# A hybrid convolution and RWKV-7 block on one Trainium2 core: scan products in one array shape, the state on VectorE, the forward substitution on GpSimd

## The chip, the cores and the metric

The kernel runs on one core of one Trainium2 chip. A core has TensorE (PE in the profile), VectorE (DVE), ScalarE (ACT), GpSimd (POOL) and SyncE (SP, here only a queue of DMA issues). Each engine works through its own instructions in the order in which they were put there, and waits for another engine at a semaphore. The metric is the device time of one execution in microseconds, the median of several runs.

## The reference

The input is x, 512 tokens of 1024 channels; 16 learned meta tokens are put ahead, so 528 tokens run through one layer of float32 arithmetic:

```python
p = h @ w_in                                  # GLU columns | r, k, v, low-rank downs | two gates
A = conformer_conv(p[:, :2048])               # GLU, causal depthwise convolution (31 taps), LN, swish, projection
B = rwkv7_time_mix(p[:, 2048:5408])           # scan, per head: S = S diag(w) + (S a) b^T + v k^T ;  y = S r
h = LN(alpha * h + (sigmoid(gA) * A + sigmoid(gB) * B) @ w_o)
h = LN(alpha * h + conv_gated_mlp(h))         # up 2 x 2816, depthwise convolution (3 taps), gate, down
```

The scan has 16 heads of 64 values. In it a is the normalised key with a minus sign, and b the normalised key times a learned rate.

## The kernel before, in words

Every large product is a `gemm` (lines 157 to 162): weights and activations are split into a high and a low part, and three products are accumulated for each of eight 128-row slices, at L160, L161 and L162. Weights come by SP's DMA queue (L146); ScalarE makes the high part (L137), VectorE the low one (L140, tile wl).

The scan runs over eight pairs of heads, and in a pair over nine chunks of 64 tokens; chunk 0 holds the 16 meta tokens. `rkv` (part K) projects r, k and v of a pair. `prep` (part P) forms decays, the matrices AR and BK, the squared norms of the keys (nsc, tokens on partitions) and the scores Gt of each chunk (L408, masked at L409). A score product contracts over the 64 channels of one head, so it has 64 rows by 128 columns of the array; the profile prints that as 64*128. ScalarE then scales Gt by the key norms (L412). The decay and rate products of the low-rank weights wup (L336, L346) also use 64 rows each.

`solve` (part S) inverts a triangular matrix for every chunk. The blocks go through DRAM (dA) into one block per partition, L and W. VectorE makes 31 steps of two instructions each (L475 a product, L477 a sum), and each needs the one before; 15 single instructions do the same for chunk 0 (L481). Between dependent steps the code puts instructions of the depthwise convolution (L647, L655). The result goes back through DRAM (dT). `merge` (L499 on) transposes a block (L512) and makes the remaining block with two sets of TensorE products (L517, L522). `chain` (L525 on) then goes through the chunks in order; every step has products of TensorE at L530 and evictions of ScalarE: R (L548), UV (L552), the state St (L559) and Y (L564). The state is decayed by one more product with the identity matrix. `finish` normalises the output, `glu` and `gate` are more gemms, and `conv` is the depthwise convolution on VectorE.

The string `SCHEDULE` lists the parts in the order in which they are put to a scheduler, for instance `C0 K2 F0 G2 S12`: `S12` is the solve of pair 1 with the convolution of tile 2 between its steps. The scheduler settles one fixed order of instructions per engine before anything runs. `front()` gives the chain and evictions a high priority, `back()` a low one. PSUM has three banks for gemms (ps_g), two for the chain (ps_x), two for scores and transposes (ps_a) and one for the rest (ps_m).

## Time and profile before

| | before |
|---|---|
| three runs, us | 1223.47, 1225.12, 1210.57 (median 1223.47) |
| profiled execution, us | span 1223.2 |
| PE busy | 1186.4 us, 97% |
| DVE busy | 844.0 us, 69% |
| ACT busy | 605.0 us, 49% |
| POOL busy | 60.8 us, 5% |
| stage with the scans, 100 to 640 us | PE 534.91 of 540.00 us |

The profiled execution takes as long as the median run: its span of 1223.2 us is 0.3 us below it. A matmul that starts while the one ahead is still draining counts as busy in both, so PE's share says little of how dense its work is; starts of successive matmuls do. A float32 product is two records in the trace, a gemm product one. The times of matmuls are given with the array shape that they use (128*128, 64*128, 64*64) and the moving tile.

### The profile page before, as it was taken

Reading aid. Unit: us, or ns where it says so; the run is one execution under the profiler, and the core shown is the slowest. Engines: PE = TensorE matmul, PEld = TensorE weight load, DVE = VectorE, ACT = ScalarE, POOL = GpSimd, SP = SyncE. Lnnn points to the kernel's source line nnn. Section 1 sums busy time; section 2 is a strip of 40 time slices with the busy share of each in tenths; the row PEclk is TensorE's granted clock in tenths of the full one; section 3 lists DMA queues with packets and bytes.
Section 4 is the critical chain, followed back from the end, with each engine's and each line's share of the span. In section 5 each row is a group of like instructions: output and inputs, shape, how many; then the busy total and the mean of one; then the engine's idle time right before and its main releaser. Section 6 shows DMA issues by size and latency. Waiting matters only on the chain.

```text
span 1223.2 us, 22803 instructions
## 1 busy us (share of the span) xinstructions
PE 1186.4 (97%) x8790; PEld 1079.5 (88%) x8790; DVE 844.0 (69%) x2103; ACT 605.0 (49%) x1407; POOL 60.8 (5%) x204
## 2 busy tenths in 40 slices
PE   5999999999999999999999998998999999999997
PEld 4998988898888888878888898998999999998885
DVE  7598967887788877877377345688877666662227
ACT  3445365556676757656677633336533443441211
POOL 5001010100101000000100000000000000000000
PEclk9999998998999999989999998999999999999999
DMA  5323331332324132342454285641332332334221
GB/s 154 87 76 88 98 76 46 82 84 61 72 63 96 47 69 62 81 110 65 94 170 116 80 231 168 178 115 53 104 104 85 88 104 82 93 107 132 89 86 69
DMA packets 200391, 118.21 MB, mean 97 GB/s; under 512 B 49524, under 2 KB 184349, under 8 KB 200283
## 3 DMA queue, kind: packets, MB, share of 16 engines
q1 hardware_dynamic: 180944, 113.03, 32.9%
q10 hardware_dynamic: 17515, 3.17, 1.5%
q8 instruction: 69, 1.13, 0.4%
q0 software_dynamic: 1824, 0.57, 0.2%
q14 instruction: 39, 0.32, 0.1%
HBM read 101.45 MB, written 15.28 MB: 95 GB/s over the span
## 4 chain that ended last, share of the span: by engine, by line
PE 82%; DVE 7%; DMA 6%; ACT 3%; issue 1%; ACTq 0%; SPq 0%; DVEq 0%
PE ps_g L160 18%; PE ps_g L161 17%; PE ps_g L162 17%; PE ps_x L530 10%; PE ps_a L408 3%; PE psf L894 3%; PE psf L896 3%; PE psf L895 3%; DMA wr<-in_w_o_dram 2%; DVE wl L140 2%; ACT wh L137 1%; DMA o_t<-o_dr 1%; PE ps_a L336 1%; PE ps_x L604 1%; DMA t<-dT 1%
## 5 line engine op out<-in xcount | busy, mean ns | idle before, releaser
L160 PE MATMUL ps_g<-hhi,wh 128*128 128x256 f32 (+2 forms) x1648 | 480.6, 292 | 3.1 <-ACT hhi L137 1.7
L161 PE MATMUL ps_g<-hhi,wl 128*128 128x256 f32 (+2 forms) x1648 | 478.9, 291 | 0.0
L162 PE MATMUL ps_g<-hlo,wh 128*128 128x256 f32 (+2 forms) x1648 | 476.5, 290 | 0.0
L160 PEld LDWEIGHTS ps_g<-hhi,wh 128*128 128x128 f32 x1648 | 314.3, 191 | 12.0 <-issue 3.4
L162 PEld LDWEIGHTS ps_g<-hlo,wh 128*128 128x128 f32 x1648 | 313.7, 191 | 7.8 <-issue 3.7
L161 PEld LDWEIGHTS ps_g<-hhi,wl 128*128 128x128 f32 x1648 | 313.9, 190 | 7.0 <-issue 2.0
L140 DVE TENSOR_TENSOR wl<-wr,wh 128x1024 fp32r<-128x1024 f32 x151 | 184.2, 1221 | 111.3 <-ACT wh L137 110.8
L137 ACT CAST wh<-wr 128x1024 fp32r<-128x1024 f32 x151 | 158.0, 1047 | 126.3 <-PE psf L895 75.2
L655 DVE SCALAR_TENSOR_TENSOR cev<-cd,drv,cev 128x257 f32<-128x257 f32 x216 | 98.0, 475 | 0.0
L852 ACT COPY pu<-ps_g 128x258 f32<-128x258 f32 (+1 forms) x88 | 33.0, 375 | 109.5 <-PE ps_g L162 109.4
L894 PE MATMUL psf<-wh,hidh 128*128 128x512 f32 x176 | 69.3, 394 | 0.0
L896 PE MATMUL psf<-wl,hidh 128*128 128x512 f32 x176 | 69.0, 392 | 0.0
L895 PE MATMUL psf<-wh,hidl 128*128 128x512 f32 x176 | 68.3, 388 | 0.0
L859 DVE SCALAR_TENSOR_TENSOR u<-pu,prm,u 128x512 f32<-128x512 f32 x88 | 65.7, 748 | 1.3
L530 PE MATMUL ps_x<-UV,Gt 128*64 128x64 f32 (+1 forms) x576 | 64.2, 235 | 0.0
L530 PEld LDWEIGHTS ps_x<-UV,Gt 128*64 128x64 f32 (+1 forms) x576 | 44.7, 137 | 17.8 <-issue 0.7
L647 DVE SCALAR_TENSOR_TENSOR csh<-cpad,drv,csh 128x257 f32<-128x257 f32 x120 | 57.6, 480 | 1.2
L552 ACT ACTIVATE UV<-ps_x,nsc 64x64 f32<-64x64 f32 x144 | 37.1, 304 | 37.7 <-PE ps_x L530 37.3
L559 ACT ACTIVATE S<-ps_x,lc 64x64 f32<-64x64 f32 x128 | 39.5, 309 | 30.4 <-PE ps_x L530 28.8
L475 DVE TENSOR_TENSOR stmp<-L,W 128x60 f32<-128x60 f32 (+24 forms) x248 | 50.5, 204 | 4.3 <-DMA L<-dA 1.6
L477 DVE TENSOR_TENSOR W<-W,stmp 128x60 f32<-128x60 f32 (+24 forms) x248 | 50.4, 203 | 2.5
L412 ACT ACTIVATE Gt<-ps_a,nsc 64x64 f32<-64x64 f32 x144 | 34.7, 304 | 32.9 <-DVE Gt L409 29.6
(279 smaller groups left out, 1985.8 us busy)
## 6 DMA issues: line engine op xcount, KB each, us to landing
wr<-in_w_in_dram SPq DMA_DIRECT2D x59, 512.0 KB, 4.1
wr<-in_ffn_up_dram SPq DMA_DIRECT2D x44, 512.0 KB, 3.9
wr<-in_ffn_down_dram SPq DMA_DIRECT2D x22, 512.0 KB, 3.6
wr<-in_w_o_dram SPq DMA_DIRECT2D x10, 512.0 KB, 4.7
g_dr<-gt SPq DMA_DIRECT2D x16, 257.0 KB, 2.9
L<-dA SPq DMA_DIRECT2D x32, 128.0 KB, 3.8
wr<-in_w_conv_out_dram SPq DMA_DIRECT2D x8, 512.0 KB, 4.2
wr<-in_w_rwkv_out_dram SPq DMA_DIRECT2D x8, 512.0 KB, 5.2
```

The source lines that it names most:

```text
L137: S.copy(out=dst_hi, in_=src)
L140: V.tensor_tensor(out=dst_lo, in0=src, in1=dst_hi.bitcast(F32), op=ALU.subtract)
L160: TE.matmul(ps, wh[:, k, :], xh(k, sl), start=(k == 0), stop=False)
L161: TE.matmul(ps, wl[:, k, :], xh(k, sl), start=False, stop=False)
L162: TE.matmul(ps, wh[:, k, :], xl(k, sl), start=False, stop=(k == nk - 1))
L530: mm = lambda o, l, r, start: TE.matmul(o, l, r, start=start, stop=True, skip_group_check=True)
L647: yield V.scalar_tensor_tensor(out=cs_, in0=x1[:, i:i + NM], scalar=dcol(D_SCW, 8 * i + j) if i < HT else dcol(D_HCW, 8 * 2 * i + j), in1= ...
L655: yield V.scalar_tensor_tensor(out=yp[:, b, :] if lasttap else ev[:, b, :], in0=d[:, i:i + NM], scalar=dcol(D_HCW, 8 * (2 * i + b) + j), i ...
L859: V.scalar_tensor_tensor(out=u, in0=p_[:, t:t + SEQ], scalar=pcol(C_FW, 44 * t + m), in1=u, op0=ALU.mult, op1=ALU.add)
L894: TE.matmul(acc[t][d], hidh[:, k, ts], wd[k][0][:, ds], start=(k == 0), stop=False)
L895: TE.matmul(acc[t][d], hidl[:, k, ts], wd[k][0][:, ds], start=False, stop=False)
L896: TE.matmul(acc[t][d], hidh[:, k, ts], wd[k][1][:, ds], start=False, stop=(k == NF - 1))
```

## The change

It does five things. The line numbers of the changed kernel differ; they are given where needed.

1. The three kinds of scan products that used 64*64 or 128*64 of the array (keys, R to U, Y) now contract over all 128 rows, with zeros in the half that does not count, and have 66 stationary columns. Gt rows are widened to 132 columns for that (GW), two buffers Rz and the upper half of UV are zeroed.
2. The state is kept by VectorE: one scalar_tensor_tensor from PSUM per head and chunk. The identity product goes. GpSimd multiplies AR with the decay (ARd).
3. The key norms are folded into BK before the scores: GpSimd spreads the reciprocals (nsb), TensorE transposes them, VectorE multiplies. ScalarE no longer scales Gt, UV or St.
4. Y is gathered from two places of PSUM, one copied by ScalarE and one added by VectorE.
5. The forward substitution moves to GpSimd, the small one for chunk 0 too. The convolution is put to the scheduler by itself, at low priority.

```diff
-    def solve(pr, extra=()):
+    def solve(pr):
...
-        def step(s):
+        tmp0 = sp.tile([32, 16], F32, name="stmp0")
+        for s in range(31):
             nj, m = s // 4 + 1, 31 - s
             tv = tmp[:, 0:nj * m].rearrange("p (j t) -> p j t", t=m)
-            yield V.tensor_tensor(out=tv, in0=L[:, s, s + 1:32].unsqueeze(1).broadcast_to([P, nj, m]),
-                                  in1=W[:, 0:nj, s:s + 1].broadcast_to([P, nj, m]), op=ALU.mult)
-            yield V.tensor_tensor(out=W[:, 0:nj, s + 1:32], in0=W[:, 0:nj, s + 1:32], in1=tv, op=ALU.add)
...
-        between, prev = chain_(small(), extra), None
-        for s in range(31):
-            for ins in step(s):
-                if prev is not None:
-                    behind(ins, prev, "work between dependent steps")
-                prev = next(between, None)
...
+            G.tensor_tensor(out=tv, in0=L[:, s, s + 1:32].unsqueeze(1).broadcast_to([P, nj, m]),
+                            in1=W[:, 0:nj, s:s + 1].broadcast_to([P, nj, m]), op=ALU.mult)
+            if s < 15:
+                G.tensor_tensor(out=tmp0[:, 0:15 - s], in0=L0[:, s, s + 1:16],
+                                in1=W0[:, s:s + 1].broadcast_to([32, 15 - s]), op=ALU.mult)
+            G.tensor_tensor(out=W[:, 0:nj, s + 1:32], in0=W[:, 0:nj, s + 1:32], in1=tv, op=ALU.add)
+            if s < 15:
+                G.tensor_tensor(out=W0[:, s + 1:16], in0=W0[:, s + 1:16], in1=tmp0[:, 0:15 - s], op=ALU.add)
         G.dma_start(out=dT0, in_=W0)
```

In `prep`, the norms and the scores:

```diff
-        V.reciprocal(out=nsc, in_=nsc)
...
+        nsb = ra.tile([P, 5, 2, HD], F32, name="nsb")
+        G.tensor_copy(out=nsb[0:66, 0], in_=nsc[0:66, 0, :].unsqueeze(2).broadcast_to([66, 2, HD]))
+        G.tensor_copy(out=nsb[:, 1:5], in_=nsc[:, 1:5, :].unsqueeze(3).broadcast_to([P, 4, 2, HD]))
+        for g0, g1, c0, c1 in ((0, 3, 0, 5), (3, 5, 5, NCH)):
...
+                TE.transpose(pt[:, t0 - 64 * c0:t1 - 64 * c0], nsb[0:t1 - t0, i].rearrange("p h n -> p (h n)"),
+                             ident[0:t1 - t0, 0:t1 - t0])
+            V.tensor_tensor(out=BK[:, c0:c1, 0:64], in0=BK[:, c0:c1, 0:64],
+                            in1=pt[:, 0:64 * (c1 - c0)].rearrange("p (c t) -> p c t", t=64), op=ALU.mult)
...
+        G.tensor_tensor(out=ARd[:, 1:NCH, :], in0=AR[:, 1:NCH, :],
+                        in1=lc[:, 0:NCH - 1].unsqueeze(2).broadcast_to([P, NCH - 1, P]), op=ALU.mult)
...
-                for c in range(c0, c1):
-                    S.activation(out=Gt[0:64, h, c, 0:64], in_=pt[0:64, P * (c - c0):P * (c - c0) + 64],
-                                 func=AF.Copy, scale=nsc[0:64, c, h:h + 1])
...
+        for c0, c1 in ((0, 1), (1, 5), (5, 9)):
+            pts = [abank(), abank()]
+            for c in range(c0, c1):
+                for h in range(2):
+                    o = pts[h][:, P * (c - c0):P * (c - c0 + 1)]
                     TE.matmul(o, BK[64 * h:64 * h + 64, c, :], AR[64 * h:64 * h + 64, c, :], start=True, stop=True)
```

In `chain`:

```diff
-                mm(X[0:64, half[h]], Gt[64:128, h, c, 0:64], UV[64:128, c, half[h]], start and h == 0)
+                mm(X[0:66, at(0, h)], Gt[:, h, c, 0:66], UV[:, c, half[h]], start and h == 0)
...
-                if c > 0:
-                    mm(Xn[:, 2 * P:3 * P], ident, St, True)
-                    keys(Xn, c + 1, False)
...
+                mm(X[0:66, at(1, h)], Gt[:, h, c, 0:66], R[:, half[h]], False)
+            S.copy(out=UV[0:64, c, :], in_=X[0:64, P:2 * P])
...
+                        V.scalar_tensor_tensor(out=o, in0=Sb[(c - 1) % 2][half[h], half[h]],
+                                               scalar=lc[half[h], c - 1:c], in1=n, op0=ALU.mult, op1=ALU.add)
             for h in range(2):
-                mm(X[64:128, half[h]], Gt[:, h, c, 64:128], UV[:, c, half[h]], c == 0 and h == 0)
...
+                mm(X[0:66, at(3, h)], Gt[:, h, c, 66:132], UV[:, c, half[h]], False)
+            if c > 0:
+                V.tensor_tensor(out=yo, in0=yo, in1=X[0:64, 3 * P:4 * P], op=ALU.add)
```

What the scheduler made of it is seen in the order of each engine. First TensorE, around the merge of pair 0 and the scores of pair 1. Before (L408 with BK_1548 are scores of pair 1, L517 and L522 the merge of pair 0):

```order
L408 MATMUL ps_a_1617<-AR_1547,BK_1548 128x128 x4
L161 MATMUL ps_g_2378<-hhi_100,wl_2374 128x272
L421 MATMUL ps_a_1630<-ident_69,BK_1548 128x128
L160 MATMUL ps_g_2405<-hhi_100,wh_2373 128x256
L517 MATMUL ps_m_1675<-t11n_1669,a21_539 128x32 x4
L522 MATMUL ps_m_1682<-t22_540,pp_1680 32x128 x4
```

Now (L524 and L529 are the merge of pair 0, L542 its chain, L425 with BK_1570 the scores of pair 1):

```order
L161 MATMUL ps_g_1875<-hhi_100,wh_1843 128x256
L524 MATMUL ps_m_1693<-t11n_1687,a21_539 128x32 x4
L529 MATMUL ps_m_1700<-t22_540,pp_1698 32x128 x4
L542 MATMUL ps_x_1715<-UV_961,Gt_928 66x64 x2
L542 MATMUL ps_x_1715<-Rz1_544,Gt_928 66x64 x2
L542 MATMUL ps_x_1730<-UV_961,BT_960 128x128
L542 MATMUL ps_x_1730<-Sb1_546,ARd_884 128x128
L425 MATMUL ps_a_1615<-AR_1568,BK_1570 128x128
L425 MATMUL ps_a_1616<-AR_1568,BK_1570 128x128
```

The merge of a pair stood behind the next pair's scores; now it stands ahead of them, so fewer gemms lie between a pair's scores and its own merge. The two heads' scores (banks 1615 and 1616) now stand next to each other in places.

Second GpSimd, for the solve of one pair. Before, it had a few issues and memsets for it:

```order
L450 DMA dA_3233<-Gt 16x2x16
L461 DMA L_3245<-dA_3233 16x256 x2
L414 MEMSET Gt 32x18x32
L465 MEMSET W 128x256
L468 MEMSET W 32x8 x4
L493 DMA dT_3235<-W_3246 32x16
L510 DMA Gt<-dT_3235 16x2x16
L469 COPY W_3969<-w_init 32x16
```

Now it holds 30 small steps (the first two and the last stand here), the round trip of chunk 0, and then 62 large steps (four stand here):

```order
L467 DMA dA_2197<-Gt 16x2x16
L478 DMA L_2209<-dA_2197 16x256 x2
L495 TENSOR_TENSOR stmp_2230<-L_2209,W_2210 32x15
L499 TENSOR_TENSOR W_2210<-W_2210,stmp_2230 32x15
L499 TENSOR_TENSOR W_2210<-W_2210,stmp_2230 32x1
L500 DMA dT_2199<-W_2210 32x16
L517 DMA Gt<-dT_2199 16x2x16
L434 MEMSET UV 64x1152
L492 TENSOR_TENSOR stmp<-L,W 128x31
L497 TENSOR_TENSOR W<-W,stmp 128x31
L492 TENSOR_TENSOR stmp<-L,W 128x76
L497 TENSOR_TENSOR W<-W,stmp 128x8
```

The large substitution starts behind the small one and behind the waits of its two DMAs, in one queue.

Third ScalarE, at the end of the solve of pair 1 in the changed kernel (in brackets the semaphores that an instruction waits for; L502 is the issue of dT):

```order
L615 ACTIVATE on<-ps_x,prm 128x2 [waits PE_49]
L502 DMA dT<-W 256x1x32 [waits DMAHW5_49,Pool_49]
L616 ACTIVATE on<-ps_x,prm 128x512 [waits PE_49]
L502 DMA dT<-W 256x1x32
L561 COPY Rz_543<-ps_x 64x128 [waits PE_49,Activation_49]
L566 COPY UV<-ps_x 64x128 [waits PE_49]
L512 DMA t22s<-dT 128x4x32 [waits DMAHW6_49,DMAHW5_49,DMAHW7_49,DMAHW4_49,DMAHW0_49]
L199 ACTIVATE k<-ps_g,prm 128x272 [waits PE_49]
L199 ACTIVATE k<-ps_g,prm 128x255 [waits PE_49]
```

The issue of dT, which waits for GpSimd, stands ahead of the copies of chunk 0 of the chain (L561, L566) and of the next pair's evictions (L199).

## Rows read from the trace of the kernel before

**Rows 1.** Stretches: length, then busy us (instructions) per engine, PE clock, DMA share, GB/s.

```profile
100.00:640.00 540.00, 534.91 (x3998) 466.50 (x3997) 415.93 (x1354) 333.22 (x913) 39.75 (x130) 0.97 0.33 82
201.80:208.60 6.80, 6.80 (x23) 5.01 (x22) 4.12 (x22) 3.85 (x7) 0.00 (x0) 0.50 0.33 85
```

**Rows 2.** Waits of PE over the span: total us, times, longest.

```profile
PE ps_m L517 <- DVE t11n L512: 3.2, 3, 1.6
```

**Rows 3.** PE timeline (start us, us, line, names, shape, count): 128*128 scan products among gemms.

```profile
419.56 0.29 PE L161 MATMUL ps_g<-hhi,wl 128*128 128x272 f32 x1
419.69 0.38 PE L530 MATMUL ps_x<-S,AR 128*128 128x128 f32 x2
419.82 0.37 PE L162 MATMUL ps_g<-hlo,wh 128*128 128x272 f32 x1
420.03 0.29 PE L160 MATMUL ps_g<-hhi,wh 128*128 128x272 f32 x1
```

**Rows 4.** PE timeline: 64*64 scan products among gemms, and three close together.

```profile
170.61 0.28 PE L162 MATMUL ps_g<-hlo,wh 128*128 128x256 f32 x1
170.82 0.44 PE L530 MATMUL ps_x<-R,Gt 64*64 64x64 f32 x4
171.20 0.40 PE L160 MATMUL ps_g<-hhi,wh 128*128 128x272 f32 x1
171.43 0.29 PE L161 MATMUL ps_g<-hhi,wl 128*128 128x272 f32 x1
...
179.48 0.33 PE L530 MATMUL ps_x<-R,Gt 64*64 64x64 f32 x3
```

**Rows 5.** The line L530: min/median/max ns of its R,Gt products.

```profile
L530 PE MATMUL ps_x<-R,Gt x255: 218/218/366, 115.0 to 640.0; 64*64 64x64 f32 x128
```

**Rows 6.** PE timeline: wup products of two row groups next to each other.

```profile
73.36 0.49 PE L336 MATMUL ps_a<-lx,wup 64*128 64x272 f32 x1
73.37 0.49 PE L346 MATMUL ps_a<-lx,wup 64*128 64x272 f32 x1
73.70 0.39 PE L336 MATMUL ps_a<-lx,wup 64*128 64x272 f32 x1
```

**Rows 7.** Timelines around pair 1: first score, last solve step, merge.

```profile
152.59 0.48 PE L408 MATMUL ps_a<-AR,BK 64*128 64x128 f32 x2
240.80 0.17 DVE L477 TENSOR_TENSOR W<-W,stmp 128x8 f32<-128x8 f32 x1
249.61 1.08 PE L517 MATMUL ps_m<-t11n,a 128*128 128x32 f32 x8
```

**Rows 8.** POOL and DVE timelines: memsets in a row, a copy beside DVE, a copy alone.

```profile
161.98 0.59 POOL L468 MEMSET W<- 32x8 f32 x4
182.72 1.28 DVE L655 SCALAR_TENSOR_TENSOR cev<-cd,drv,cev 128x257 f32<-128x257 f32 x3
183.69 0.36 POOL L469 COPY W<-w_init 32x16 f32<-32x16 f32 x1
470.65 0.21 POOL L469 COPY W<-w_init 32x16 f32<-32x16 f32 x1
```

**Rows 9.** Groups by form: busy us, mean ns of one, idle before.

```profile
L331 POOL MEMSET E<- 128x585 f32 x8 | 4.7, 591 | 68.2 <-DVE AR L365 40.8 <-PE ps_m L243 25.9 <-ACT r L198 1.6
L468 POOL MEMSET W<- 32x8 f32 x32 | 3.4, 107 | 1.7
L655 DVE SCALAR_TENSOR_TENSOR cev<-cd,drv,cev 128x257 f32<-128x257 f32 x216 | 98.0, 475 | 0.0
L475 DVE TENSOR_TENSOR stmp<-L,W 128x60 f32<-128x60 f32 x24 | 5.2, 215 | 0.3
```

**Rows 10.** DMA issues: KB each, median us from issue to landing.

```profile
L<-dA POOLq DMA_DIRECT2D x16, 16.0 KB, 1.9
dA<-Gt POOLq DMA_DIRECT2D x8, 2.0 KB, 1.8
dT<-W POOLq DMA_DIRECT2D x8, 2.0 KB, 2.2
```

More of the change, by code (lines that the diff above doesn't have):

```diff
@@ L523, in merge @@
         S.copy(out=Gt[0:32, :, 1:9, 32:64], in_=pt[0:32, :].rearrange("p (h c t) -> p h c t", h=2, t=32))
+    Rz = [sp.tile([P, P], F32, name=f"Rz{i}") for i in range(2)]
+    Sb = [sp.tile([P, P], F32, name=f"Sb{i}") for i in range(2)]
+    for t_ in Rz + Sb:
+        G.memset(t_, 0.0)
     def chain(pr):
@@ L539, in chain @@
         for c in range(NCH):
+            y0 = 0 if c % 2 == 1 else 64
+            yo = Y[y0:y0 + 64, (c + 1) // 2, :]
             if c > 0:
-                mm(X[:, 0:P], pr["AR"][:, c, :], St, False)
+                mm(X[:, 0:P], pr["AR"][:, c, :], Sb[(c - 1) % 2], False)
+                keys(X, c, False)
+            R = Rz[c % 2]
+            S.copy(out=R[0:64, :], in_=X[0:64, 0:P])
+            if c > 0:
+                S.copy(out=yo, in_=X[64:128, 0:P])
+            for h in range(2):
+                mm(X[0:66, at(1, h)], Gt[:, h, c, 0:66], R[:, half[h]], False)
@@ L542, in chain @@
+            S.copy(out=UV[0:64, c, :], in_=X[0:64, P:2 * P])
             if c < NCH - 1:
                 Xn = xbank()
-                if c > 0:
-                    mm(Xn[:, 2 * P:3 * P], ident, St, True)
-                    keys(Xn, c + 1, False)
-            R = sp.tile([64, P], F32, name="R", bufs=3)
-            S.copy(out=R, in_=X[0:64, 0:P])
-            for h in range(2):
-                mm(X[0:64, P + 64 * h:P + 64 * h + 64], Gt[0:64, h, c, 0:64], R[:, half[h]], False)
-            for h in range(2):
-                S.activation(out=UV[0:64, c, half[h]], in_=X[0:64, P + 64 * h:P + 64 * h + 64], func=AF.Copy,
-                             scale=pr["nsc"][:, c, h:h + 1])
@@ L563, in chain @@
-            y0 = 0 if c % 2 == 1 else 64
-            S.copy(out=Y[y0:y0 + 64, (c + 1) // 2, :], in_=X[64:128, 0:P])
+                mm(Xn[:, 2 * P:3 * P], pr["BT"][:, c, :], UV[:, c, :], True)
+                for h in range(2):
+                    o, n = Sb[c % 2][half[h], half[h]], Xn[half[h], at(2, h)]
+                    if c == 0:
+                        S.copy(out=o, in_=n)
+                    else:
+                        V.scalar_tensor_tensor(out=o, in0=Sb[(c - 1) % 2][half[h], half[h]],
+                                               scalar=lc[half[h], c - 1:c], in1=n, op0=ALU.mult, op1=ALU.add)
@@ L725, in hybrid_block @@
         elif what == "S":
-            solved[p] = solve(prs[p], conv(q, cpads.pop(q)) if q >= 0 else ())
+            solved[p] = solve(prs[p])
+            if q >= 0:
+                with back():
+                    for _ in conv(q, cpads.pop(q)):
+                        pass
         elif what == "C":
```

62 lines of the change are left out of this document (27 added, 35 removed).

## The prediction

> **What bounds the kernel now.** I read the stretches first. From 100 to 640 us, the stage with the scans, TensorE is busy for 534.91 of 540.00 us, VectorE for 415.93, ScalarE for 333.22 and GpSimd for 39.75 [rows 1]. The reader should see that three engines have room and one has none. Next the waits: the merge of a pair, where TensorE needs the result of the forward substitution, costs it 3.2 us in all [rows 2]. So the substitution, long as it is, hides behind gemms. How long the cover is shows in the timelines around pair 1: first score at 152.59, last step at 240.80, merge at 249.61 [rows 7]. The cover is 97 us, and the way back through DRAM to the merge takes 9 us.
>
> Third, what the scan costs TensorE, read from starts of matmuls. In 128*128 shape, a visit of two records among gemms of 272 columns goes from 419.56 to 420.03 [rows 3]. Two gemm records take 0.125 each (0.13 and 0.12 between starts), which leaves 0.22: 0.11 a record and nothing for the visit. In 64*64 shape, a visit of four records goes from 170.61 to 171.43 [rows 4], 0.82; less one gemm record of 256 and one of 272 columns (0.24) that is 0.57. Records of this shape packed together start every (0.33 - 0.22) / 2 = 0.056 us [rows 4, 5], so four are worth 0.23, and 0.34 goes to the two changes of array shape, 0.17 each.
>
> **The change, part by part.** Sums are made against the profiled execution, 1223.2 us, which is the median of the runs to 0.3 us.
>
> *TensorE.* Counted in the orders of instructions, changes of array shape fall from 568 to 242: 326 x 0.17 = 55 us saved. The identity product goes: 56 products are 112 records, x 0.112 = 12.5 saved. The recast products have 66 stationary columns for 64, so I let a record cost 0.06; over the chain that adds 0.8. If an array shape of 128 columns cost a record 0.112 whatever its columns, it would add 46; I take the lower value since these records are nearest in columns to those of 64, and keep the other as a rival. Two heads' scores next to each other use separate row groups, and such products start 0.01 apart [rows 6]; this holds for 30 of 72 couples, saving two records of 0.112 each, 6.7. For the wup products 7 more couples stand so, and each saves two records of 0.33 [rows 6]: 4.5. The 40 new transposes cost 0.11 each, 4.4 more. Together 55 + 12.5 - 0.8 + 6.7 + 4.5 - 4.4 = **73.5 us less work for TensorE**, all in the stage that it bounds.
>
> *VectorE and ScalarE.* VectorE loses 62 substitution steps a pair of about 0.2 us [rows 9] and gains state, Y and norm work of about half as much; ScalarE loses the scalings. Both were covered by TensorE and stay so; I cost this at nothing. If TensorE's cover went, ScalarE's copies in the chain would be next on the path.
>
> *The substitution.* It becomes a path of its own on GpSimd, each instruction waiting for the one ahead. No row has a GpSimd product of two inputs, so I bound it. From below: a copy of 16 elements alone takes 0.21 [rows 8]; memsets grow by (591 - 107) / (585 - 8) = 0.84 ns an element [rows 9], so 31 further elements read from two inputs add 0.05 (the mean step has 47); four memsets in 0.59 with 0.107 each [rows 8, 9] leave 0.055 between instructions. That gives 0.32, of which a step on VectorE would have 0.215 [rows 9]. From above: the same copy takes 0.36 when it starts under a VectorE operation with two inputs in SBUF, ending 0.05 us after the last of three in a row [rows 8]; if every step had to wait for one such operation, 0.475 [rows 9], it would be 0.53. I take **0.36 + 0.055 = 0.415 us a step**, from the row that shows GpSimd reading beside the convolution, since the convolution now runs through without steps between its instructions.
>
> The Trainium skill's GPSIMD Engine Reference (Elementwise, side-by-side cycle accounting) has about 2.6 cycles an element for a two-input operation at 1.2 GHz, which speaks against moving this work off VectorE. By an estimate from it the 31 further elements cost 0.067 instead of 0.05 us, 1 us over a pair's 62 steps; no run here shows such an operation yet.
>
> *The path of a pair*, from its first score: 1.5 us for the scores and mask of chunk 0; DMAs of chunk 0 through DRAM, landing in 1.8 and 1.9 [rows 10], with three issues and the semaphores between about 8 in all so far; 30 small steps, between 0.265 and 0.415, at 0.30 each 9; then, ahead of the large steps in the same queue, a landing of 2.2 [rows 10], two issues, the copy and memsets, about 5. So the large steps start at 22, end at 22 + 62 x 0.415 = 47.7, and with the 9 us back [rows 7] the merge can start at **56.7 us**.
>
> *The cover.* In the new order the merge of a pair no longer stands behind the next pair's scores, so less lies between. Counted with the prices above, TensorE's work from first score to merge is 37, 62, 58, 42, 49, 46, 56 and 43 us for pairs 0 to 7. The same count on the old order gives 77 to 94, and 94 for pair 1 where the trace has 97. Where work is shorter than 56.7, TensorE waits: 19.6, -, -, 15.0, 7.5, 10.9, -, 13.9.
>
> In pairs 1, 2 and 6 another wait comes sooner. ScalarE's issue of dT waits for GpSimd, and queued behind it are the copies of chunk 0 of the chain and evictions of gemms. TensorE reaches the product that needs those copies 37.4, 35.2 and 43.6 us after the first score, by the same count, and stands until 47.7; what then remains before the merge (24, 23, 13 us) is more than 9, so it loses 10.3, 12.5 and 4.1. All eight sum to **93.8 us**.
>
> *Clock.* In this stage there is a stretch of 6.8 us at a granted clock of 0.50, 1.2 GHz instead of 2.4, in which TensorE has 23 matmuls; it fell with no wait of TensorE on record [rows 1]. Waits of 10 us may bring more such stretches, and denser work take some away; I put both at nothing, within 10 us either way.
>
> Sum: 1223.2 - 73.5 + 93.8 = **1244 us**. 2% of the median, what a measurement here can tell from no change, is 24.5: the bounds are 1199 and 1248. My value is just inside.
>
> **The rivals.** *Forecast, 0.55:* the saving comes, and TensorE then waits for the substitution at the merge, as above. Its own range is path lengths from 51 to 66 us: 1199 (waits of 50) to 1318 (168).
>
> *Cheap steps, 0.27.* GpSimd's steps run as alone, and the convolution seldom holds them up. With a solve end at 39 us and a path of 48 the waits are 10.9, 1.6, 3.8, 6.3, 0, 2.2, 0 and 5.2, 30 in all: **1180 us**. It decides below a path of 51 us, that is 0.32 a step or less and short small steps. For it: 0.21 for a copy alone. Against it: one copy is one sample, and reads one input where a step reads two.
>
> *The shared way into SBUF holds every step, 0.09.* Each large step waits for one convolution operation, 0.53, and each small one too: 22 + 7 + 33 + 9 = 71 us. Waits are then 208 us: **1358 us**, slower. It decides once VectorE has two-input work behind each step, and has it from about 0.45 us a step on. For it: the copy of 0.36. Against it: by counts of rows such work fills about a third of the time. The Trainium skill's page SBUF — State Buffer (Who interferes with whom) has GpSimd and VectorE exclude each other for the whole instruction when VectorE has two SBUF inputs; the row of 0.36 agrees, and by it VectorE would be held up in turn, which no row shows.
>
> *The recast does not do what it is for, 0.06.* If the 66-column records cost 0.112, TensorE's saving is 27 instead of 73.5; some 4 us a pair of it lies under the cover and shortens the waits by 25: 1244 + 46 - 25 = 1265 us. Against it stand the 0.056 of 64-column records.
>
> The rest, 0.03, is a result that none of these give.
>
> **How the numbers follow.** Faster by over 2%: the cheap steps, 0.27. Within 2%: paths from 51 to 57 us, 0.22 of the forecast's 0.55, and the rest, together 0.25. Slower: the forecast's other 0.33, with 0.09 and 0.06, 0.48. The predicted time is that of the likeliest case, 1244. The range reaches down to 1175, a path of 47 us, and up to 1325, a path just over 66; outside lie the cheapest steps and the case in which every step is held.
>
> **What would show it.** Steps of about 0.36 us on GpSimd in groups of 62, 0.41 between starts; TensorE waiting at the merge (now L524) on the DVE transpose in pairs 0, 3, 4, 5 and 7 for 8 to 20 us each, and in pairs 1, 2 and 6 on ScalarE's copies of R or on evictions; scan products of 66 columns without the gap of 0.34 around a visit; records about 0.06 apart. The prediction is wrong if steps start less than 0.3 or more than 0.5 us apart, if merges are reached without a wait, or if TensorE's work in the stage falls by much less than 70 us.

## The result, and the profile after

The changed kernel takes 1311.72 us, the median of four runs from 1308.96 to 1314.66; the kernel before takes 1224.3, the median of four. The ratio is 1.0734, with an interval of 1.0660 to 1.0808: slower, by some 87 us where 20 were forecast. The profiled execution has a span of 1307.3 us, 84.1 more than before. First the page's engines:

```profile
PE 1155.3 (88%) x8718; PEld 1065.8 (82%) x8718; DVE 825.8 (63%) x1679; ACT 526.8 (40%) x1083; POOL 326.8 (25%) x968
```

Then the stretches of the changed kernel, in the columns of [rows 1]: the stage with the scans, and one piece of pair 1.

```profile
100.00:640.00 540.00, 433.99 (x3338) 387.52 (x3337) 339.10 (x815) 223.63 (x542) 260.78 (x781) 0.89 0.26 62
203.70:224.20 20.50, 8.54 (x37) 7.24 (x38) 2.02 (x6) 2.04 (x7) 9.06 (x36) 0.50 0.18 37
```

Against [rows 1] TensorE is busy for 433.99 of 540.00 us instead of 534.91, and no engine has taken its place: VectorE and ScalarE are less busy too, and GpSimd, which now makes the substitution, is idle for half of the stage. So the stage is bounded by waits that pass from engine to engine. The waits of TensorE from 80 to 740 us (total, times, longest) show where it stands still:

```profile
PE ps_x L542 <- ACT Rz L561: 43.9, 4, 15.0
PE ps_x L542 <- ACT Sb L573: 29.2, 3, 14.5
PE ps_x L621 <- ACT on L616: 14.6, 1, 14.6
PE ps_a L337 <- ACT E L341: 10.8, 1, 10.8
PE ps_x L542 <- DMA Gt<-dT: 9.7, 1, 9.7
...
PE ps_m L524 <- DVE t11n L519: 1.4, 1, 1.4
```

All the large ones but one name ScalarE, with four different products of it; the merge, where the forecast had most of its wait, costs 1.4 us, and 2.2 more in a wait for nsc. That ScalarE is not itself slow is seen in its timeline. The rows are in order of time (start, duration, line, names, and in brackets the idle time before): L497 is GpSimd's last step of pair 1, L502 ScalarE's issue of dT, L616 its next work (Y L541 in its bracket is a memset of GpSimd, right behind that last step), the rest the matmuls of TensorE that start after a long wait, and two of the merges.

```profile
147.59 0.79 PE L337 MATMUL ps_a<-lx,wup 64*128 64x256 f32 x1 [10.76 <-ACT E L341]
213.95 0.21 POOL L497 TENSOR_TENSOR W<-W,stmp 128x8 f32<-128x8 f32 x1
...
214.19 0.59 ACTq L502 DMA_DIRECT2D dT<-W  x1
214.83 0.78 ACT L616 ACTIVATE on<-ps_x,prm 128x512 f32<-128x512 f32 x1 [16.30 <-POOL Y L541]
...
215.66 1.22 PE L621 MATMUL ps_x<-lg,gup 128*128 128x256 f32 x2 [14.65 <-ACT on L616]
245.29 1.08 PE L524 MATMUL ps_m<-t11n,a 128*128 128x32 f32 x8
309.18 1.24 ACTq L502 DMA_DIRECT2D dT<-W  x2
312.09 0.71 PE L542 MATMUL ps_x<-Rz,Gt 128*66 128x64 f32 x4 [14.95 <-ACT Rz L561]
334.79 0.97 PE L524 MATMUL ps_m<-t11n,a 128*128 128x32 f32 x8
400.39 0.71 PE L542 MATMUL ps_x<-Rz,Gt 128*66 128x64 f32 x4 [15.01 <-ACT Rz L561]
479.33 0.77 PE L542 MATMUL ps_x<-Sb,ARd 128*128 128x128 f32 x2 [14.46 <-ACT Sb L573]
557.95 0.77 PE L542 MATMUL ps_x<-Sb,ARd 128*128 128x128 f32 x2 [14.03 <-ACT Sb L573]
630.75 0.71 PE L542 MATMUL ps_x<-Rz,Gt 128*66 128x64 f32 x4 [4.66 <-ACT Rz L561]
714.03 0.71 PE L542 MATMUL ps_x<-Rz,Gt 128*66 128x64 f32 x4 [9.28 <-ACT Rz L561]
```

These are eight waits, one for each pair, and together 97.8 us. Each ends 0.5 to 3 us behind an issue of dT on ScalarE, which itself waits for GpSimd's last step: in pair 1 that step ends at 214.16, ScalarE issues at 214.19, makes `on` at 214.83 after 16.30 us without work, and TensorE goes on at 215.66. Whatever stood behind the issue in ScalarE's queue (`on`, E, Rz or Sb) became late. The merges come up to 30 us later and nearly all without a wait.

By the records of all matmuls the 84.1 us divide as follows. TensorE's idle time ahead of matmuls, in pieces of over 0.4 us, grows from 25.9 to 139.8 us, +114. TensorE is busy for 59.5 us at half clock instead of 32.5; if half of that is lost, an estimate, it costs 29.8 us instead of 16.2, +13. What is left, the work itself with the short waits, falls by 43, where 73.5 had been forecast.

### The profile page after: what moved, and what is told of

It reads as the page before. It is cut to its first block, busy times and chain, and to the rows that moved or that the text cites. A ratio compares the mean times of both kernels' runs of the same rounds, so it can differ in the third digit from the quotient of the medians.

```text
span 1307.3 us, 22770 instructions
## 1 busy us (share of the span) xinstructions
PE 1155.3 (88%) x8718; PEld 1065.8 (82%) x8718; DVE 825.8 (63%) x1679; ACT 526.8 (40%) x1083; POOL 326.8 (25%) x968
## 4 chain that ended last, share of the span: by engine, by line
PE 63%; POOL 16%; DVE 6%; DMA 5%; issue 5%; ACT 3%; ACTq 1%; SPq 0%; POOLq 0%; DVEq 0%
PE ps_g L161 14%; PE ps_g L162 14%; PE ps_g L163 14%; POOL W L497 6%; POOL stmp L492 6%; PE ps_x L542 5%; PE psf L916 3%; PE psf L918 3%; PE psf L917 3%; POOL stmp L495 2%; PE ps_a L425 1%; POOL W L499 1%; DMA L<-dA 1%; DVE wl L141 1%; DMA dA<-Gt 1%
## 5 line engine op out<-in xcount | busy, mean ns | idle before, releaser
L161 PE MATMUL ps_g<-hhi,wh 128*128 128x256 f32 (+2 forms) x1648 | 482.7, 293 | 5.7 <-ACT hf_t L268 3.9
L161 PEld LDWEIGHTS ps_g<-hhi,wh 128*128 128x128 f32 x1648 | 319.3, 194 | 10.4 <-ACT hf_t L268 4.6
L163 PEld LDWEIGHTS ps_g<-hlo,wh 128*128 128x128 f32 x1648 | 318.2, 193 | 3.0 <-issue 1.9
L162 PEld LDWEIGHTS ps_g<-hhi,wl 128*128 128x128 f32 x1648 | 318.4, 193 | 2.5 <-issue 1.3
L492 POOL TENSOR_TENSOR stmp<-L,W 128x60 f32<-128x60 f32 (+24 forms) x248 | 85.3, 344 | 22.4 <-DMA L<-dA 3.9
L497 POOL TENSOR_TENSOR W<-W,stmp 128x60 f32<-128x60 f32 (+24 forms) x248 | 85.2, 343 | 19.3
L542 PE MATMUL ps_x<-Rz,Gt 128*66 128x64 f32 x288 | 33.8, 243 | 46.9 <-ACT Rz L561 43.9
L542 PEld LDWEIGHTS ps_x<-Rz,Gt 128*66 128x66 f32 x288 | 24.9, 147 | 58.9 <-ACT Rz L561 45.4
L542 PE MATMUL ps_x<-UV,Gt 128*66 128x64 f32 x576 | 60.5, 229 | 10.8 <-DMA Gt<-dT 9.7
L561 ACT COPY Rz<-ps_x 64x128 f32<-64x128 f32 x72 | 18.6, 259 | 127.4 <-PE ps_x L542 76.7
L542 PEld LDWEIGHTS ps_x<-UV,Gt 128*66 128x66 f32 x576 | 55.5, 145 | 12.3 <-DMA Gt<-dT 9.9
```

The costliest lines, as they stand in the source:

```text
L161: TE.matmul(ps, wh[:, k, :], xh(k, sl), start=(k == 0), stop=False)
L162: TE.matmul(ps, wl[:, k, :], xh(k, sl), start=False, stop=False)
L163: TE.matmul(ps, wh[:, k, :], xl(k, sl), start=False, stop=(k == nk - 1))
L492: G.tensor_tensor(out=tv, in0=L[:, s, s + 1:32].unsqueeze(1).broadcast_to([P, nj, m]), in1=W[:, 0:nj, s:s + 1].broadcast_to([P, nj, m]), o ...
L497: G.tensor_tensor(out=W[:, 0:nj, s + 1:32], in0=W[:, 0:nj, s + 1:32], in1=tv, op=ALU.add)
L542: mm = lambda o, l, r, start: TE.matmul(o, l, r, start=start, stop=True, skip_group_check=True)
```

## The experiments

"Theory A" below is that the substitution on GpSimd makes the loss; B, that the rest of the change does. Ratios are to the kernel before, with their intervals.

**The substitution back on VectorE, all else as changed (e1), and the reverse: the kernel before with the substitution alone on GpSimd (e2).**

```diff
-            G.tensor_tensor(out=tv, in0=L[:, s, s + 1:32]...
+            yield V.tensor_tensor(out=tv, in0=L[:, s, s + 1:32]...
...
-            solved[p] = solve(prs[p])
-            if q >= 0:
-                with back():
-                    for _ in conv(q, cpads.pop(q)):
-                        pass
+            solved[p] = solve(prs[p], conv(q, cpads.pop(q)) if q >= 0 else ())
```

> The changed kernel with the forward substitution back on VectorE between the taps of the convolution, as before; all else of the change stays. Theory A, TensorE waits for the path over GpSimd: in the new order 72, 80, 87, 83, 85, 85, 71 and 49 us of TensorE's work lie between first score and merge, so the long waits (some 113 us more than before) go, the half clock goes with them, and what is left is the recast's saving of about 44 us: 1180 us, 1165 to 1195. Theory B, the recast chain itself makes the waits, since its state now goes over VectorE and its copies queue on ScalarE: the waits at R and at the state stay, 1270 us or more.

> The kernel before with its forward substitution alone moved to GpSimd, the convolution by itself; scan products, norms and state as before. 44, 73, 65, 50, 60, 50, 67 and 51 us of TensorE's work lie between first score and merge. Theory A: the substitution ends about 49 us after the first score, the merge can start 9 or more later, and ScalarE's issue of dT holds back evictions; long waits of 40 to 90 us, half clock behind them, 1265 to 1320 us. Theory B: the chain is the old one, so no new waits, 1223 us within 2%.

e1: 1231.98 us, 1.0094 (1.0053 to 1.0134). e2, with these lines the other way round: 1327.3 us, 1.0889 (1.0798 to 1.0979), 7 us above its range. A holds: the substitution on GpSimd costs 80 us in the changed kernel (1311.7 - 1232.0), and alone it costs as much and more. Both edits move the place of the convolution in VectorE's order along with it; e4 below leaves that place alone. But e1 is not at 1180 either. All that was to make TensorE's work less brings nothing as a whole, so a second cause is to be found.

**Every second large step left out (e4), and 40 of 46 convolution instructions of a tile left out (e5).**

```diff
+            if s % 2 == 0:
+                G.tensor_tensor(out=tv, ...)
...
+            if s % 2 == 0:
+                G.tensor_tensor(out=W[:, 0:nj, s + 1:32], ...)
```

```diff
-        for i in range(1, HT + 1):
-            yield V.scalar_tensor_tensor(out=cs_, in0=x1[:, i:i + NM], ...)
...
-        for i in range(HT + 1):
+        for i in (0, HT - 1, HT):
```

> The changed kernel with every second of the 31 large steps left out (their product and sum), so the substitution is not whole; 33, 61, 60, 41, 47, 36, 59 and 38 us lie between first score and merge. Theory A: the path is 30 steps of 0.42 us shorter, 12.6 us, its end about 36 us after the first score in place of 49, and each pair's wait falls by about as much: 1307 - 8 x 10 = 1225 us, 1205 to 1245. Theory B: waits of the chain do not depend on it, above 1285 us.

> The changed kernel with 40 of the 46 instructions of each convolution tile left out, so that VectorE seldom reads two inputs from SBUF while GpSimd works. Theory A alone: GpSimd's steps are as long as they are by themselves, 0.34 us and 0.42 between starts, and the time stays at 1290 to 1310. Theory C, GpSimd waits for VectorE at the shared way into SBUF: steps fall to below 0.28, 0.35 between starts, the path by 5 us or more per pair, and the time by 40 us or more, to 1265 or less.

Each of these two ran once. e4: 1245.58 us; the last step comes 35 to 42.5 us behind the first score instead of 49 to 54, and 66 us of the loss are gone. So most of the price hangs on the number of dependent steps. e5 takes away most of the convolution that VectorE makes beside GpSimd, and still takes 1284.31 us, between what the two theories gave. The two costliest GpSimd groups (busy us, mean ns, idle before), first of the changed kernel, then of e5:

```profile
L492 POOL TENSOR_TENSOR stmp<-L,W 128x60 f32<-128x60 f32 (+24 forms) x248 | 85.3, 344 | 22.4 <-DMA L<-dA 3.9
L497 POOL TENSOR_TENSOR W<-W,stmp 128x60 f32<-128x60 f32 (+24 forms) x248 | 85.2, 343 | 19.3
```

```profile
L492 POOL TENSOR_TENSOR stmp<-L,W 128x60 f32<-128x60 f32 (+24 forms) x248 | 82.1, 331 | 26.1 <-DMA L<-dA 7.6
L497 POOL TENSOR_TENSOR W<-W,stmp 128x60 f32<-128x60 f32 (+24 forms) x248 | 81.1, 327 | 19.2
```

A step falls from 344 to 331 ns and no further. Contention with the convolution is not what makes it long; GpSimd's own instructions are. The shorter steps are worth 7 us over all pairs (85.3 + 85.2 - 82.1 - 81.1); where the other 20 of e5's 27 us come from is not shown.

**The issues of dT and t22s off ScalarE's queue (e3).** If the wait at ScalarE were only one of place, this would remove it.

```diff
-            (nc.sync, nc.scalar)[q % 2].dma_start(out=dT...
+            nc.sync.dma_start(out=dT...
...
-        nc.scalar.dma_start(out=t22s, in_=dT[1]...
+        nc.sync.dma_start(out=t22s, in_=dT[1]...
```

> The changed kernel with all four issues of dT and the load behind them on SP's queue instead of two on ScalarE's, so ScalarE no longer stands behind GpSimd; 40, 62, 58, 44, 50, 48, 56 and 42 us of TensorE's work lie between first score and merge. Theory G, ScalarE's wait at dT is where most of the waits come from: the large steps end 51 to 54 us after the first score as before, the merge can start 9 us later, waits are then about 90 in place of 120 us and stand at the merge itself: 1275 to 1290 us. Rival: SP's queue stands in its place and holds back weights: 1305 us or more.

1310.11 us, 1.0708 (1.0656 to 1.0759): nothing gained. Its waits of TensorE:

```profile
PE ps_m L524 <- DVE t11n L519: 44.0, 4, 15.4
PE ps_x L608 <- ACT Y L604: 12.9, 3, 12.4
PE ps_a L399 <- POOL nsb L393: 11.3, 1, 11.3
PE ps_g L162 <- DVE wl L141: 10.3, 2, 9.5
```

Much of the wait now stands at the merge (L524), where the forecast had put it, and the rest at other products of VectorE, ScalarE and GpSimd. ScalarE no longer issues dT, but it stands for 86.7 us, in seven waits, at its copy of t22s, which needs the same result, and VectorE for 80.9 us, in six, at the transpose t11n.

**Where the recast's gain went: the copy of Y behind the copy of UV (e6, on e1); besides that the small steps on GpSimd (e8); besides that Y over 128 columns, without VectorE's add (e9).**

```diff
-            if c > 0:
-                S.copy(out=yo, in_=X[64:128, 0:P])
...
+            if c > 0:
+                S.copy(out=yo, in_=X[64:128, 0:P])
```

```diff
-                yield V.scalar_tensor_tensor(out=W0[:, s + 1:16], in0=L0[:, s, s + 1:16], ...
+            G.tensor_tensor(out=tmp0[:, 0:15 - s], in0=L0[:, s, s + 1:16], ...
+            G.tensor_tensor(out=W0[:, s + 1:16], in0=W0[:, s + 1:16], in1=tmp0[:, 0:15 - s], op=ALU.add)
```

```diff
-                mm(X[0:66, at(3, h)], Gt[:, h, c, 66:132], UV[:, c, half[h]], False)
-                V.tensor_tensor(out=yo, in0=yo, in1=X[0:64, 3 * P:4 * P], op=ALU.add)
+                mm(X[:, at(0, h)], Gt[:, h, c, 2:130], UV[:, c, half[h]], c == 0 and h == 0)
+            S.copy(out=yo, in_=X[64:128, 0:P])
```

> The kernel of e1 (recast, substitution on VectorE) with ScalarE's copy of the first part of Y put behind its copy of UV, so that the product R to U has only the copy of R ahead of it. In e1 a visit of scan products costs 0.195 us more than its own records, 34.5 us over 177 visits, and the trace names ScalarE's copy of Y 52 times ahead of it. Theory D, the product waits for both copies: the excess falls below 0.12 a visit, 10 to 20 us less than e1, 1212 to 1222. Theory F, the products of 66 columns in a 128*128 shape cost this by themselves: excess and time as in e1, 1232 within 6.

> e6 with the 15 small steps of chunk 0 on GpSimd, which takes about 24 us off VectorE. Theory E, VectorE is the second bound (459 of 540 us busy in e1's stage, 416 before) and its lateness makes the 36 us of long waits that e1 has more than the kernel before: the waits fall by 10 to 25 us against e6, about 1200. If VectorE is not what is late: as e6.

> e8 with the Y product over 128 stationary columns that adds up in the place where the state's part of Y lies, so VectorE's 64 additions (18 us) and one of two copies go, and TensorE has 288 records of 0.11 instead of 0.06, 15 us more. Theory E: the lighter VectorE pays for about that, within 10 us of e8. Theory F: no difference from e8 but the 15 us.

e6: 1224.61 us, 1.0053 (1.0010 to 1.0095), 7 us less than e1. e8: 1249.73, 1.0261 (1.0199 to 1.0323), 25 us more than e6 where less was expected. e9: 1241.51, 1.0192 (1.0130 to 1.0253). The rows of weight loads (PEld) tell what e6 was about. A load waits in the chain for ScalarE's copy of Y, in the changed kernel and in e1:

```profile
PEld ps_x L542 <- ACT Y L563: 11.2, 39, 0.9
```

```profile
PEld ps_x L551 <- ACT Y L572: 12.6, 52, 0.4
```

Waits of 0.2 to 0.3 us, many of them, are what the recast has uncovered. Measured as the time by which a visit of scan products exceeds its own records (and 0.17 for each change of shape), it is 0.02 us a visit before, 0.21 in the changed kernel, 0.195 in e1 and 0.155 in e6: putting Y later helps, by less than expected, and the intervals of e1 and e6 overlap. In e6 the loads' waits for Y fall to 1.6 us (six times), and those for R (Rz) rise from 1.0 to 5.6 us (23 times). e8's loss was not foreseen and I leave its cause open; its largest wait is 17.5 us in four pieces, at gemms (L161) that wait for VectorE's work on v. e9 is 8 us below e8, within what was expected.

**One part of the rest at a time, on the kernel before: the shapes alone (e10; the keys' products of a chunk also move there from the step before into the chunk's own), shapes and norms (e11), shapes and the state on VectorE (e12), shapes and the two heads' scores next to each other (e13), and e13 with the norms (e14).** Of each a line or two:

```diff
-                mm(X[0:64, half[h]], Gt[64:128, h, c, 0:64], UV[64:128, c, half[h]], start and h == 0)
+                mm(X[0:66, half[h]], Gt[:, h, c, 0:66], UV[:, c, half[h]], start and h == 0)
```

```diff
-                    S.activation(out=Gt[0:64, h, c, 0:64], ..., scale=nsc[0:64, c, h:h + 1])
+            V.tensor_tensor(out=BK[:, c0:c1, 0:64], in0=BK[:, c0:c1, 0:64], in1=pt..., op=ALU.mult)
```

```diff
-                    mm(Xn[:, 2 * P:3 * P], ident, St, True)
+                        V.scalar_tensor_tensor(out=o, in0=Sb[(c - 1) % 2][half[h], half[h]], ...
```

```diff
-                pt = abank()
+            pts = [abank(), abank()]
...
+                for h in range(2):
+                    o = pts[h][:, P * (c - c0):P * (c - c0 + 1)]
```

> The kernel before with only the shapes recast: keys and R to U with 66 columns, Y with 128 columns, zeros where needed. State with the identity product on TensorE, norms on ScalarE, substitution on VectorE as before, so VectorE has no new work. Changes of array shape fall from 568 to 219: 349 x 0.17 = 59 us saved, the wider records cost 16. Theories D and E, the recast does save and other parts of the change took it back: 1224 - 43 = 1181, 1170 to 1197. Theory F, the recast itself does not save: 1215 or more.

> e10 with the key norms folded into BK as in the change (spread by GpSimd, 40 transposes, 16 multiplications on VectorE), ScalarE's scalings gone. By the counts TensorE has 4 us more. Theory E, work added ahead of the scores on GpSimd and VectorE is late: 8 us or more above e10's 1206. If ScalarE's load mattered: at or below 1206.

> e10 with the state on VectorE and the identity product gone, AR decayed by GpSimd, as in the change. TensorE has 112 records of 0.112 less, 12.5 us, VectorE about 31 us more in a stage in which e10 has it busy for 436 of 540. Theory E, VectorE's lateness takes the saving: 1200 to 1215. If VectorE has room: e10 less 12, about 1193.

> e10 with the scores of the two heads next to each other as in the change. In the changed kernel's trace such neighbours save one record of 0.11 each time, not two; some 30 of them are 3 us. Expected 1202, 1196 to 1207; if the pairs of score banks taken at once hold TensorE up, above 1208.

> e13 with the norms folded into BK as in e11: recast shapes, scores of the two heads next to each other, folded norms; state on TensorE and ScalarE and substitution on VectorE as before. e13 was at 1191, and e11 was 4 us below e10. If the parts add up: 1187, 1180 to 1194; this would be the fastest.

| | us | ratio (95%) |
|---|---|---|
| e10, shapes | 1205.58 | 0.9885 (0.9855 to 0.9915) |
| e11, shapes and norms | 1201.28 | 0.9812 (0.9760 to 0.9864) |
| e12, shapes and state | 1230.02 | 1.0039 (1.0003 to 1.0076) |
| e13, shapes and heads | 1190.87 | 0.9728 (0.9673 to 0.9783) |
| e14, shapes, heads and norms | 1203.35 | 0.9913 (0.9875 to 0.9950) |

Only e13 is with its whole interval more than 2% from the kernel before; the others lie closer to it. The shapes alone save 17 us and not 43. Putting two heads' scores together saves 15 more, against some 3 that were expected. In e13's trace 54 records of scores start within 0.03 us of the one ahead; at 0.11 each that is 6 us, and the rest is not explained. And **e13 beats both kernels by a ratio that the measurement can tell**. The state on VectorE costs 24 us although it removes an identity product for each chunk: in e12 TensorE waits for the merge's transpose, which stands in VectorE's queue, in a row that e13 has at 1.6 us. That is some 10 of the 24 us.

```profile
PE ps_m L524 <- DVE t11n L519: 12.4, 3, 10.2
```

The parts do not add up: the norms bring 4 us on e10, where the intervals overlap, and cost 12 on e13. Each part makes the scheduler settle another order, and some of what is measured may be that order; no run shows it apart. In e13's stage, in the columns of [rows 1], TensorE starts 222 more matmuls than in [rows 1] at about the same busy time, so the work is denser:

```profile
100.00:640.00 540.00, 533.06 (x4220) 484.81 (x4218) 442.38 (x1403) 355.94 (x961) 49.10 (x142) 0.99 0.34 88
```

**Can the substitution on GpSimd be hidden? The old cover given back: merge and chain of a pair behind the next pair's scores, on the changed kernel (e15) and on e14 with the substitution on GpSimd (e16).**

```diff
+            if pr["p"] + 1 in lastsc:
+                behind(ins, lastsc[pr["p"] + 1], "merge behind the next scores")
...
+                if c == 0 and pr['p'] + 1 in lastsc:
+                    behind(ins, lastsc[pr['p'] + 1], 'chain behind the next scores')
```

> The changed kernel with the merge of a pair and the start of its chain put behind the scores of the next pair on TensorE, as the order was before; every instruction stays where it was on the other engines' programs, GpSimd has the substitution. 51, 80, 73, 64, 69, 61, 63 and 38 us lie between first score and merge instead of 37 to 62. Theory H, it is the cover that the change lost and not the engine: with a path of 61 us waits of 10 and 23 us are left, and 1312 falls to 1240, 1220 to 1265. Rival: any pair loses as before, since ScalarE and SP stand behind GpSimd whatever the order: 1290 or more.

> e14 with the substitution on GpSimd and the merge behind the next pair's scores, covers of 51, 83, 75, 68, 67, 63, 67 and 38 us. Theory H: waits of some 35 us against e14, less what a lighter VectorE gives back: 1205 to 1230. Rival: 1260 or more.

e15: 1300.01 us, 1.0713 (1.0644 to 1.0783). e16: 1297.57, 1.0699 (1.0615 to 1.0782). TensorE's work from first score to merge is now 51, 80, 73, 64, 69, 61, 63 and 38 us in e15, against a path of some 61 us (51.7 to the last step, and 9 back): as much or more in six of eight pairs, and the loss stays. So a lack of cover at the merge alone is not the cause either. e15's waits of TensorE:

```profile
PE ps_x L547 <- ACT UV L573: 49.4, 8, 13.7
PE ps_x L547 <- ACT Y L570: 42.7, 11, 12.8
```

ScalarE stands at the issue of dT in the middle of the previous pair's chain, and the copies of that chain stand behind it.

**Then ScalarE's queue freed too: dT issued by GpSimd and t22s by SP, GpSimd's memsets for others on VectorE (e17, on e16), the same issues and the cover on the changed kernel (e18), and at last every consumer put behind the previous pair's finish (e19, on e17).**

```diff
-            (nc.sync, nc.scalar)[q % 2].dma_start(out=dT...
+            G.dma_start(out=dT...
...
-        nc.scalar.dma_start(out=t22s, in_=dT[1]...
+        nc.sync.dma_start(out=t22s, in_=dT[1]...
```

```diff
-        nc.sync.dma_start(out=t11, ...
+        G.dma_start(out=t11, ...
...
+            behind(tr, done[pr["p"] - 1][0], "merge behind the finish ahead")
...
+                behind(tc_, done[pr["p"] - 1][1], "merge behind the finish ahead")
```

> e16 with nothing of other engines behind GpSimd's substitution: GpSimd issues dT itself, SP loads t22s, and the memsets of E, th, k, v, r, Y, S and cpad go to VectorE. Covers of 50, 84, 74, 67, 68, 62, 68 and 40 us. In e16 TensorE's long waits were still 100 us, now behind ScalarE's copies in the middle of the chain of the pair before, and at E. Theory I, cover alone or a free ScalarE alone only move the wait, both together remove it: 1205 to 1235. Rival: waits as in e16, 1285 or more.

> The same two edits (cover as in e15, nothing behind GpSimd's substitution as in e17) on the changed kernel itself, with its state, Y and norms. Theory I: most of the long waits go, 1300 falls to 1215 to 1250, what is left above e17 being the state on VectorE. Rival: 1285 or more.

> e17 with the consumers of the substitution moved: all loads of the merge on GpSimd's own queue, and the transpose of t11 on VectorE and the copies of t22 on ScalarE behind the finish of the pair before. In e17 each of seven pairs still loses 8 to 19 us once, TensorE at the finish behind ScalarE's normalisation, ScalarE at the copies of t22 (70 us in all), VectorE at the transpose (80 us). Theory J, whichever in-order queue holds the first instruction that needs the substitution stops there, and the loss goes only when none of them is ahead of other work: waits fall by 50 us or more, 1298 to 1245 or less. Rival: the path over GpSimd is too long for a pair's period in any order: 1280 or more.

e17: 1298.93 us, 1.0694 (1.0645 to 1.0743). e18: 1306.34, 1.0751 (1.0711 to 1.0791), no gain on the changed kernel either. e17's waits, of TensorE (80 to 740 us), ScalarE and VectorE (100 to 700), show the wait handed on once more:

```profile
PE ps_x L601 <- ACT Y L597: 68.0, 6, 14.0
...
ACT t L520 <- DMA t22s<-dT: 70.1, 6, 14.5
...
DVE t11n L518 <- DMA t<-dT: 79.9, 7, 13.3
```

ScalarE no longer issues dT; it copies t22s (L520), and that copy waits for the same data in the same place of its queue, as VectorE's transpose does (L518). Behind them stands the finish of the previous pair, for which TensorE waits at L601. e19 puts these two behind that finish: 1253.49 us, 1.0275 (1.0193 to 1.0358), 45 us less than e17. Its waits of TensorE:

```profile
PE ps_a L398 <- POOL nsb L392: 20.6, 2, 19.9
PE ps_a L338 <- ACT E L342: 16.8, 3, 8.5
PE ps_m L529 <- DVE t11n L520: 7.5, 1, 7.5
```

The 68.0 us at L601 are gone, which is the theory's mark. The time lies between the theory's 1245 and the rival's 1280, so half of the loss (1298.9 against e14's 1203.4) is not removed by it. Of the 50 us left to e14, TensorE's waits of over 0.4 us between 80 and 760 us make 43 (54.4 against 11.6). The largest, 19.9 us at nsb, which GpSimd itself makes, stood in e17 with the same length. e19 moves loads, transpose and copies together, so it does not tell which of them counts.

## Why the prediction was wrong, point by point

**The substitution's path: right.** Its two instruction groups last 344 and 343 ns, 0.42 us between starts with the gap of some 0.08; forecast were 0.36 and 0.415. Large steps started 21.9 to 26.3 us behind the first score, and ended at 49.0 to 54.3, 51.7 in the mean, where 47.7 stood, 4 us sooner. The cheap steps (0.32 or less) and the steps that are all held (0.53) fall, and e5 speaks against the second too. One held step is seen in the trace of the changed kernel (start, duration): VectorE's wl covers a step of 30 elements, which takes 1.23 us where the next of its line takes 0.24.

```profile
190.54 1.22 DVE L141 TENSOR_TENSOR wl<-wr,wh 128x1024 fp32r<-128x1024 f32 x1
...
190.62 1.23 POOL L492 TENSOR_TENSOR stmp<-L,W 128x30 f32<-128x30 f32 x1
191.93 0.24 POOL L497 TENSOR_TENSOR W<-W,stmp 128x30 f32<-128x30 f32 x1
192.25 0.24 POOL L492 TENSOR_TENSOR stmp<-L,W 128x29 f32<-128x29 f32 x1
```

The Trainium skill's page SBUF — State Buffer (Who interferes with whom) says that the two engines exclude each other for a whole instruction when VectorE reads two inputs from SBUF; this row agrees. Of the 496 instructions of the large steps 29 last over 0.6 us, 15 of them under a wl; together they cost some 2.5 us a pair against the shortest of their form. In e5, which leaves wl as it is, there are 34. So e5 bounds what contention with the convolution costs a step, at 13 to 16 ns, and not what wl costs it.

**TensorE's saving of 73.5 us: wrong, and the first failed step.** The work fell by 43. A saving by changes of shape was priced as if a visit cost its records and its switches. Two pieces of PE's timeline of the changed kernel (columns as in [rows 3]), the first with ScalarE's copy of Y and the weight load behind it, show what came instead:

```profile
420.16 0.28 PE L161 MATMUL ps_g<-hhi,wh 128*128 128x272 f32 x1
420.20 0.26 ACT L563 COPY Y<-ps_x 64x128 f32<-64x128 f32 x1
420.51 0.31 PEld L542 LDWEIGHTS ps_x<-Rz,Gt 128*66 128x66 f32 x4 [0.28 <-ACT Y L563]
420.51 0.45 PE L542 MATMUL ps_x<-Rz,Gt 128*66 128x64 f32 x4
420.77 0.37 PE L162 MATMUL ps_g<-hhi,wl 128*128 128x272 f32 x1
420.98 0.28 PE L163 MATMUL ps_g<-hlo,wh 128*128 128x272 f32 x1
...
422.56 0.29 PE L161 MATMUL ps_g<-hhi,wh 128*128 128x272 f32 x1
422.69 0.38 PE L542 MATMUL ps_x<-Sb,ARd 128*128 128x128 f32 x2
422.91 0.40 PE L542 MATMUL ps_x<-UV,Gt 128*66 128x64 f32 x4
423.12 0.37 PE L162 MATMUL ps_g<-hhi,wl 128*128 128x272 f32 x1
423.32 0.29 PE L163 MATMUL ps_g<-hlo,wh 128*128 128x272 f32 x1
```

In the second piece 0.76 us lie between 422.56 and 423.32; less two gemm records (0.25) and two of Sb,ARd (0.22) that leaves 0.29 for four records of 66 columns, 0.072 each, without a gap: the recast works, at 0.072 instead of 0.06. The records themselves start 0.06 apart, as forecast ((0.40 - 0.22) / 3); the rest falls at the return to the gemm. In the first, 0.82 lie between 420.16 and 420.98; less 0.25 it is 0.57, to the hundredth what the visit of [rows 4] cost with its two switches. The 0.34 saved by the shape is spent: the load of Rz,Gt waits 0.28 us for ScalarE's copy of Y, a wait that the switch may have hidden before. In the kernel before, the chain's loads wait for a copy of Y once, for 0.2 us. Over all visits the excess is some 18 us (0.207 us by 97 visits, against 0.020 by 128), and the records' 0.012 by 864 is up to 10; the two overlap by some 5, since the excess is counted with records of 0.06. That is some 23 of the 30 us that are missing; the rest stays open. The heads' scores are not among it: 62 records of scores start within 0.03 us of the one ahead, which is 31 couples and the 6.7 us that were forecast. e10, e6 and the PEld rows show the waits; the shares are estimates from starts of matmuls. The recast's own extra was also worked out wrong: with the records at 0.056, as written, 864 x 0.004 is 3.5 us and not 0.8, and the sum 1246.

**The waits of 93.8 us: size nearly right, place wrong.** The eight largest, one a pair, sum to 97.8. But they were forecast at ScalarE's queue for pairs 1, 2 and 6 only, and came there in all eight; 66.9 of the 93.8 were to stand at the merge, where 3.6 stood. That the sums are so near is therefore in part luck. With 9.7 more where chunk 0 waits for its own substitution in pair 0 (L542 behind Gt<-dT), and smaller ones, all long waits grew by 114. The cover that I counted ran to the merge, the last consumer; the first one, an issue in ScalarE's queue, held TensorE up 17 to 44 us ahead of it, with other pairs' work queued behind. The prediction named this queue, but counted it in three pairs.

**VectorE and ScalarE at nothing: wrong.** No price in their busy time, but the state on VectorE costs 24 us in e12, on the kernel of e10; in the changed kernel it was not measured apart. And e3, e15 and e17 show pairs' waits standing at ScalarE's and VectorE's instructions, whichever of them comes first.

**The clock at nothing: wrong by some 13 us.** In the granted clock's record TensorE is at 0.50, 1.2 GHz, for 139.9 us between 80 and 760, against 34.1 before. Eight of its eleven stretches in that time begin inside one of the waits of over 3 us. In the stretch shown above the clock fell at 203.7, when TensorE had been waiting since 201.0, and stood at that level until 224.2, while TensorE worked again from 215.66 on. In e10, without long waits, it is 17.1 us, in e4 81.9. Here the lower clock came mostly with the waits, and added to them.

So the sum fails by 30 of TensorE's saving, 20 of waits and 13 of clock, 63 in all: 1307 against 1244. The sign was right, the likeliest case named a wait for the substitution, and the range, up to 1325, still held the result. Two of the signs of being wrong that the prediction gave came true: merges were reached without a wait, and TensorE's work fell by much less than 70 us. The largest error is that saving, to whose failing I had given 0.06, and for another reason: I thought of records of 0.112.

What the experiments settle: the substitution on GpSimd costs 80 us in the changed kernel (e1), 108 on the kernel before (e2) and 94 on e14 (e16), mostly by its number of steps (e4), not by contention with the convolution (e5), and not by one queue or by the cover alone (e3, e15 to e18). Moving its consumers behind other work takes away half of it, on e14's form of the kernel (e19); that the same would help the changed kernel was not run. What they leave open: the last 50 us between e19 and e14, where the path over GpSimd may simply be too long for a pair, e8's loss, and why the norms bring 4 us on e10 and cost 12 on e13.

## What to carry to other kernels

Where each engine has a fixed order, ask of a result that comes later where its *first* consumer stands on every queue, and what stands behind it there; the cover up to the last consumer is not enough, and taking away one wait shows the next. A gap on TensorE may be hiding a copy on another engine: look for that copy before the gap is counted as saved. And try each part of a compound change by itself, since here two of its parts, the shapes and the heads' order, were worth 2.7% and were buried under the others.

## What the runs showed of the hardware

GpSimd's products of two inputs take 0.21 us for 8 elements a partition (the row at 213.95 above) and 0.32 for 76 where it is shortest (0.38 in the mean), with some 0.08 between dependent ones. Its large product, by forms (busy us, mean ns):

```profile
L414 POOL TENSOR_TENSOR ARd<-AR,lc 128x1024 f32<-128x1024 f32 x8 | 17.3, 2167 | 8.6 <-DVE AR L367 8.6
```

That is 2.1 ns an element. The Trainium skill's GPSIMD Engine Reference (Elementwise, side-by-side cycle accounting) has 2.6 cycles at 1.2 GHz, by an estimate 2.2 ns; the row agrees. In the small steps the fixed part counts more than the element: 0.21 of a mean step's 0.34 us is there with 8 elements.

Scores of two heads next to each other start in a rhythm of 7, 207 and 6 ns. Four such records, between the same neighbours of the chain, take 0.42 us (from 167.89 in the changed kernel), where four records in the order of one head take 0.64 (from 172.04): a couple saves two records of 0.11, as the prediction had it. The expectation of e13 counted one.
